# The recurrence of a hybrid layer stack: half-array products in pairs, small inversions on GpSimd

## The chip, the cores and the metric

The kernel runs on one core of one Trainium2 chip, in one launch. The metric is the device time of one launch in microseconds; three runs of the kernel before gave 2369.61, 2371.10 and 2373.16 us, median 2371.1 us.

The engines are named as in the profile: PE is the matrix engine (TensorE, its weight loads are shown as PEld), DVE is VectorE, ACT is ScalarE, POOL is GpSimd, SP is the engine whose queue issues nearly all transfers of this kernel.

## The reference, cut to what matters

Two blocks follow each other on 256 tokens of 1024 features. The second block's first layer has a mixer with two halves: grouped attention, and a two-directional recurrence over 256 context and 256 latent tokens with 8 heads of 64 features (the two directions of a head run over the tokens in opposite order). The change lies in the recurrence alone:

```python
w_log = w0 + einsum('btdr,drc->btdc', tanh(wl), w2)      # d: the two directions, r: 64
decay = exp(-exp(-softplus(-w_log) - 0.5))
a = sigmoid(a0 + einsum('btdr,drc->btdc', al, a2))
k_dir = k * (1 + (a - 1) * k_a)
def step(S, inp):                                          # once per token, one 64x64 state per head
    r, w, k, v, kk, a = inp
    S = S * w - (S @ kk)[:, None] * (kk * a) + v[:, None] * k
    return S, S @ r
```

## The kernel before

All numbers are float32. The stack is a chain of matrix products whose weights stream from HBM; each weight tile is split into a high and a low part (`split`, L97 and L98) and each product runs as three passes (`mm3`, L115 to L117). These products fill most of the span. The recurrence lies between about 880 and 1195 us.

**Units.** The recurrence does not step through tokens. It cuts the 512 tokens into four tiles of 128, each of two chunks of 64, and works on eight units, one per tile and direction. For each unit four functions run:

- the first half of `rwkv_in` (the *front*): it loads the two low-rank inputs of the tile into `wa` (one transfer, L1463; direction 0 uses the partitions 0 to 63, direction 1 the partitions 64 to 127, `db`), multiplies with `rwkv_w2` for the decay (L1466, 64 rows of the array, 512 columns wide), sums the logarithms over the chunk with a triangular product (L1479), takes exponentials (L1481, L1482), and multiplies with `rwkv_a2` for the rate `a` (L1488, four products on the same 64 rows) followed by tanh on ACT (L1493). All three products use the one PSUM bank `fr`, one after the other;
- the second half of `rwkv_in` (the *back*): it scales keys and queries on DVE (L1507 to L1519) and then forms the 64x64 Gram matrices of eight heads in two chunks (L1529). For a chunk `ch` and a parity `q` of the head, four products on 64 rows (`half(q)`: partitions 0 to 63 or 64 to 127) write the one PSUM bank `gg`; then DVE multiplies that bank with a mask into SBUF (L1533). So there are four groups of four products per unit, two on each row half, and `gg` is filled and emptied four times. Between them `fill` puts pieces of the attention half into the program. Afterwards two sets of transposes on `gg` (L1544) are copied out by ACT (L1545);
- `rwkv_solve`: the diagonal 16x16 blocks of the Gram matrices go to HBM (`dq`, L1540), come back as 64 lanes of 16x16 (`dl`, L1560), are inverted by 14 pairs of small multiply and add (L1565, L1566: 64 partitions by at most 56 columns, each dependent on the one before; the profile shows them under the helper's line L120 with the tiles `dt` and `dl`), and go back to HBM (`dy`, L1568). The multiplies and adds are DVE's, the two transfers are SP's;
- `rwkv_maps`: it reads the blocks back (`x`, L1589), transposes them on DVE (L1590) and completes the 64x64 inverses by 64x64 products on all four quarters of the array (`each`, L1595), then builds each chunk's map of the state (`lw`, L1637, L1651). `lw` and `si` are buffers of 128x1024 that are cleared once by POOL (L1280, L1284).

Then `rwkv_step` carries the state through the chunks (L1669, L1678).

**Order.** The list `GA` (L22) writes out the order of the first units beside the projections of the same layer; `rwkv` (L1272) then runs, for each `n`: back of unit n, front of unit n+2, solve of unit n, maps of unit n-2, and steps after every second one. `rate` (L355, values `FT` and `FE`) says how many pieces of attention `fill` puts at each point. The framework then plans each engine's queue by these priorities and by when operands and buffers come free, so that the pieces of several functions alternate on an engine. Each queue runs in order; an instruction that waits holds up all behind it on its engine.

**PSUM.** Eight banks. While the recurrence runs, `fr` and `wm` have one each; `wm` serves the modulation products of other stages and is not used in this one.

Of the kernel before, what the change touches and what calls it, by code (L numbers as in the profile page):

```python
# [14 lines left out]
AF = mybir.ActivationFunctionType  # L15
# [31 lines left out]
@with_exitstack  # L47
def kernel(ctx: ExitStack, tc: tile.TileContext, A: dict, out: bass.AP, taps=None):
    nc = tc.nc
    V, S, E = nc.vector, nc.scalar, nc.tensor  # L50
    taps = taps or {}

    cpool = ctx.enter_context(tc.tile_pool(name="cpool", bufs=1))
# [1024 lines left out]
    def even_mixer(l, en):  # L1078
        T = 512
        close_psum()  # L1080
        with tc.tile_pool(name=nm("em"), bufs=1) as pk, tc.tile_pool(name=nm("rf"), bufs=2) as fp, \
                tc.tile_pool(name=nm("emd"), bufs=1, space=bass.MemoryType.DRAM) as dp:
            open_psum(fr=1, wm=1)
            open_psum(mm=3, sc=1, tr=1, gg=1)

            def dram(name, *shape):
# [1 line left out]

            D = dict(q=dram("qd", 4, 8, 128), k=dram("kd", 4, 512), vv=dram("vvd", 4, 128), o=dram("oTd", 8, 512), g=dram("gd", 4, 512), x=en.store, f=dram("fd", 12, 512), lo=dram("lod", 3, 512), v=dram("vd", 4, 512))
            rc = const("rcols", pk)  # L1090
            C = {n: const(n, pk) for n in ("rwkv_w2", "rwkv_a2", "rtri", "gmask", "tmask", "eye2", "sgn")}
            a0 = const("rwkv_a0", pk)
            C["ha0"] = pk.tile([128, 2, 4], F32, tag="ha0", name="ha0")
            ts(C["ha0"], a0, 0.5)
# [177 lines left out]
    def rwkv(C, D, order, stages, bon, yac):  # L1272
        front, back, solve = stages
        with tc.tile_pool(name=nm("rk"), bufs=1) as pk:
            eye2 = C["eye2"]
            C["lw"] = []
            for n in range(2):
                C["lw"].append([pk.tile([128, 4, 4, 64], F32, tag=f"lw{n}{ch}", name=nm("lw")) for ch in range(2)])
                for ch in range(2):
                    nc.gpsimd.memset(C["lw"][n][ch], 0.0)  # L1280
            si = []
            for n in range(2):
                x = pk.tile([128, 2, 2, 4, 64], F32, tag=f"si{n}", name=nm("si"))
                nc.gpsimd.memset(x, 0.0)  # L1284
                for par in range(2):
                    hb = half(1 - par)
                    for d in range(2):
                        acopy(x[hb, d, par], eye2[hb].unsqueeze(1).to_broadcast([64, 4, 64]))
                si.append(x)

            with tc.tile_pool(name=nm("ru"), bufs=2) as up, tc.tile_pool(name=nm("rw"), bufs=1) as wk, tc.tile_pool(name=nm("at"), bufs=1) as ap:
                stream[0] = merge(ORDER, iter(()), even_attention(D, ap, ("sc", "tr", "tr")))
                C["up"][1], C["wk"] = up, wk
                tm = gate_consts(D, pk)
                side = iter(())

                def steps(p):
                    tiles = ((2, 3), (0, 1))[p // 2]
                    z = {(un["d"], un["t"]): un["z"] for un in order[4 * (p // 2):2 * p + 2]}
                    for n in (0, 1) if p % 2 == 0 else (2, 3):  # L1300
                        yield from rwkv_step(n, tiles, z, si, yac)

                ahead = 2
                for n in range(8 + ahead):
                    rate[:] = FE.get(n, FT)
                    if n < 8:
                        for do, what in zip((back, front, solve), "bfs"):
                            u = n + 2 * (what == "f")
                            if u < 8 and (what, u) not in GA:
                                do(u)  # L1310
                    if n >= ahead:
                        u = n - ahead
                        for _ in rwkv_maps(C, D, order[u]):
                            fill(rate[3])
                            next(side, None)
                        if u % 2:
                            for _ in steps(u // 2):
                                fill(rate[4])
                            if u == 3:
                                side = itertools.chain(*(g for t in (2, 3) for g in (gates(D, bon, tm, t), readout(D, tm, t, yac[:, t % 2], True))),  # L1320
                                                       *(gates(D, bon, tm, t) for t in (0, 1)))
                for _ in side:
                    fill(FR)
                drain()
# [128 lines left out]
    def rwkv_in(fp, C, D, un):  # L1453
# [5 lines left out]
        def w512(tag, shape=(128, 4, 128), pool=fp, bufs=None):  # L1459
            return pool.tile(list(shape), F32, tag=tag, name=nm(tag), **({"bufs": bufs} if bufs else {}))  # L1460

        wa = w512("wa", (128, 2, 128))
        nc.sync.dma_start(out=wa[db], in_=D["lo"][db, 0:2, tok])  # L1463

        ps = pst("fr")
        E.matmul(out=ps, lhsT=wa[db, 0], rhs=C["rwkv_w2"][db, :], start=True, stop=True)  # L1466
        sg = w512("sg", (128, 512), bufs=1)
        nc.sync.dma_start(out=sg, in_=A["rwkv_w0"][:, d])
        tt(sg, ps, sg, ALU.add)
# [13 lines left out]
        inc, exc = eo[:, :, :, 1 - d:65 - d], eo[:, :, :, d:64 + d]  # L1483
        pc = eo[:, :, :, 64 - first]

        ps = pst("fr")
        for f in range(4):
            E.matmul(out=ps[:, f * 128:(f + 1) * 128], lhsT=C["rwkv_a2"][db, f * 128:(f + 1) * 128], rhs=wa[db, 1], start=True, stop=True)  # L1488

        ak = w512("ak", (128, 4, 4, 64))  # L1490
        at, kd = ak[:, :, 0:4:3], ak[:, :, 1:3]
        for f in range(4):
            S.activation(out=at[:, f], in_=ps[:, f * 128:(f + 1) * 128].rearrange("p (c t) -> p c t", c=2), func=AF.Tanh, scale=0.5, bias=C["ha0"][:, d, f:f + 1])  # L1493
            S.activation(out=kd[:, f], in_=at[:, f], func=AF.Identity, scale=C["kah"][:, 0, f:f + 1], bias=C["kah"][:, 1, f:f + 1])
        S.activation(out=at, in_=at, func=AF.Copy, scale=0.5, bias=0.5)
        yield
# [25 lines left out]
        g = w512("g", (128, 8, 2, 192), up)  # L1522
        for ch in range(2):
            cc = slice(ch * 64, ch * 64 + 64)
            for q in range(2):
                ps = pst("gg")
                for h in range(4):
                    f, hb = h, half(q)
                    E.matmul(out=ps[:, h * 128:(h + 1) * 128], lhsT=ak[hb, f].rearrange("p a t -> p (a t)")[:, ch * 128:ch * 128 + 128],  # L1529
                             rhs=ar[hb, f, 1:3, cc], start=True, stop=True)  # L1530
                if q or ch:
                    fill(rate[0])
                tt(g[:, q:8:2, ch, 64:192], ps.rearrange("p (h t) -> p h t", h=4),  # L1533
                   gmask[:, d, ch].unsqueeze(1).to_broadcast([128, 4, 128]), ALU.mult)
        if d == 1:
            gt = fe[:, 8:12].rearrange("p n (a t) -> p (n a) t", a=2)
# [2 lines left out]
        for ch in range(2):  # L1539
            nc.sync.dma_start(out=rows_of(dq, ch), in_=gt[half(ch)] if d == 1 else g[half(ch), :, ch, 128:192])  # L1540
        for ch in range(2):
            ps = pst("gg")
            for j in range(4):
                E.transpose(ps[:, j * 128:(j + 1) * 128], bk.rearrange("p f a t -> p f (a t)")[:, j, ch * 128:(ch + 1) * 128], ident)  # L1544
            S.activation(out=g[:, :, ch, 0:64], in_=ps.rearrange("p (h t) -> p h t", h=8), func=AF.Copy, scale=C["sgn"][:, ch:ch + 1])  # L1545
# [10 lines left out]
    def rwkv_solve(C, un):  # L1556
        wk = C["us"]

        y = wk.tile([64, 16, 16], F32, tag="dl", name=nm("dl"), bufs=2)
        nc.sync.dma_start(out=y, in_=lanes_of(un["dq"]))  # L1560
        for c in range(1, 15):
            n = 15 - c
            tmp = wk.tile([64, 64], F32, tag="dt", name=nm("dt"), bufs=2)
            o = tmp[:, :c * n].rearrange("p (a r) -> p a r", a=c)
            tt(o, y[:, 0:c, c].unsqueeze(2).to_broadcast([64, c, n]), y[:, c, c + 1:16].unsqueeze(1).to_broadcast([64, c, n]), ALU.mult)  # L1565
            tt(y[:, 0:c, c + 1:16], y[:, 0:c, c + 1:16], o, ALU.add)  # L1566
        V.memset(y.rearrange("p a r -> p (a r)")[:, 0:256:17], 1.0)
        nc.sync.dma_start(out=lanes_of(un["dy"]), in_=y)  # L1568

    def rwkv_maps(C, D, un):  # L1570
        d, t, u, dy, ar, g = (un[n] for n in ("d", "t", "u", "dy", "ar", "g"))
# [299 lines left out]
def _layout(x):  # L1871
# [35 lines left out]
    o["rows_g"] = _rows(x["q_gain_2"], x["k_gain_2"])  # L1907
    o["rwkv_mu"] = _cols(x["rwkv_mu_2"][0])
    o["rwkv_w0"] = np.broadcast_to(x["rwkv_w0_2"], (128, 2, 512))
    o["rwkv_w2"] = x["rwkv_w2_2"][0].reshape(128, 512)  # L1910
    o["rwkv_a0"] = _cols(x["rwkv_a0_2"][0])
    o["rwkv_a2"] = x["rwkv_a2_2"][0].reshape(128, 512)
    o["rwkv_g2"] = x["rwkv_g2_2"][0]
    o["rcols"] = _cols(np.stack([x["rwkv_k_k_2"][0], x["rwkv_k_a_2"][0], x["rwkv_r_k_2"][0].reshape(512)]))
    o["gn"] = np.broadcast_to(np.stack([x["rwkv_gn_w_2"][0], x["rwkv_gn_b_2"][0]]), (128, 2, 512))
# [29 lines left out]
```

## Time and profile before

| | |
|---|---|
| runs | 2369.61, 2371.10, 2373.16 us |
| profiled execution | 2372.83 us, span 2371.0 us |
| PE busy | 2272.9 us (96%), 13642 matrix instructions |
| DVE busy | 1570.0 us (66%) |
| ACT busy | 1069.8 us (45%) |
| POOL busy | 5.6 us, 10 instructions |
| mean granted clock of PE | 0.97 |

The profile is of one execution. Each float32 product shows as two PE records. The time of a stretch is given from the span's start. A record of PE has a measured start and a modelled end, so starts are what to compare. The chain is the sequence of work that ended last, followed back from the end: at each step what released it. DMA issues show on the issuing engine's queue (SPq); "to landing" is the time from the issue to the arrival of the data.

### The profile page before, as it was taken

Reading aid. Unit: us, or ns where it says so; the run is one execution under the profiler, and the core shown is the slowest. Engines: PE = TensorE matmul, PEld = TensorE weight load, DVE = VectorE, ACT = ScalarE, POOL = GpSimd, SP = SyncE. Lnnn points to the kernel's source line nnn. Section 1 sums busy time; section 2 is a strip of 40 time slices with the busy share of each in tenths; the row PEclk is TensorE's granted clock in tenths of the full one; section 3 lists DMA queues with packets and bytes.
Section 4 is the critical chain, followed back from the end, with each engine's and each line's share of the span. In section 5 each row is a group of like instructions: output and inputs, shape, how many; then the busy total and the mean of one; then the engine's idle time right before and its main releaser. Section 6 shows DMA issues by size and latency. Waiting matters only on the chain.

```text
span 2371.0 us, 35433 instructions
## 1 busy us (share of the span) xinstructions
PE 2272.9 (96%) x13642; PEld 1856.6 (78%) x13642; DVE 1570.0 (66%) x3074; ACT 1069.8 (45%) x1882; POOL 5.6 (0%) x10
## 2 busy tenths in 40 slices
PE   8999999999999998998878999999999999999998
PEld 6688797778787786876767878787778788768998
DVE  7867779667835766878678677437754334787555
ACT  6756666322224637564535222224422223476444
POOL 0000000000000000000000000000000000000000
PEclk9999998999999998999979999999999999999999
DMA  8556444545524445332354555323553222314553
GB/s 294 176 183 218 164 154 161 188 162 182 180 94 130 144 147 141 90 87 60 92 189 140 169 181 183 124 91 120 175 183 132 90 98 90 103 36 136 181 184 118
DMA packets 161962, 342.02 MB, mean 144 GB/s; under 512 B 48513, under 2 KB 76161, under 8 KB 161665
## 3 DMA queue, kind: packets, MB, share of 16 engines
q1 hardware_dynamic: 161072, 339.15, 43.7%
q8 instruction: 108, 1.77, 0.3%
q10 hardware_dynamic: 720, 0.60, 0.1%
q14 instruction: 62, 0.50, 0.1%
HBM read 321.86 MB, written 17.84 MB: 143 GB/s over the span
## 4 chain that ended last, share of the span: by engine, by line
PE 89%; DVE 5%; ACT 3%; DMA 1%; issue 1%; SPq 0%; DVEq 0%; ACTq 0%
PE mm L115 25%; PE mm L117 24%; PE mm L116 24%; PE gg L1529 2%; PE m L1595 1%; PE tr L219 1%; PE m L1651 1%; DVE wlo L98 1%; PE wm L331 1%; PE po L1056 1%; PE wm L274 1%; PE tr L1056 1%; ACT whi L97 1%; PE po L541 1%; PE sc L1010 1%
## 5 line engine op out<-in xcount | busy, mean ns | idle before, releaser
L97 ACT CAST whi<-raw 128x1024 fp32r<-128x1024 f32 (+2 forms) x437 | 437.4, 1002 | 988.9 <-PE mm L116 596.1
L115 PE MATMUL mm<-xh,whi 128*128 128x512 f32 (+1 forms) x1912 | 680.8, 360 | 16.5 <-ACT xh L97 9.5
L117 PE MATMUL mm<-xh,wlo 128*128 128x512 f32 (+1 forms) x1912 | 679.2, 357 | 5.2 <-DVE wlo L98 5.0
L116 PE MATMUL mm<-xl,whi 128*128 128x512 f32 (+1 forms) x1912 | 680.4, 357 | 1.2 <-DVE xl L98 1.1
L98 DVE TENSOR_TENSOR wlo<-raw,whi 128x1024 fp32r<-128x1024 f32 (+2 forms) x437 | 507.5, 1163 | 256.0 <-ACT whi L97 249.5
L115 PEld LDWEIGHTS mm<-xh,whi 128*128 128x128 f32 x1912 | 365.1, 192 | 82.2 <-ACT whi L97 16.4
L117 PEld LDWEIGHTS mm<-xh,wlo 128*128 128x128 f32 x1912 | 365.3, 191 | 57.8 <-DVE wlo L98 7.1
L116 PEld LDWEIGHTS mm<-xl,whi 128*128 128x128 f32 x1912 | 365.4, 191 | 53.8 <-DVE xl L98 4.2
L117 PE MATMUL mm<-hh,wlo 128*128 128x512 f32 (+1 forms) x704 | 260.0, 369 | 0.0
L116 PE MATMUL mm<-hl,whi 128*128 128x512 f32 (+1 forms) x704 | 258.0, 367 | 0.1
L115 PE MATMUL mm<-hh,whi 128*128 128x512 f32 (+1 forms) x704 | 257.0, 366 | 0.0
L129 DVE SCALAR_TENSOR_TENSOR macc<-raw,modc,macc 128x1024 f32<-128x1024 f32 x189 | 234.3, 1278 | 0.5
L129 DVE SCALAR_TENSOR_TENSOR xres<-mm,mod,xres 128x256 f32<-128x256 f32 x216 | 96.2, 479 | 167.1 <-PE mm L117 166.8
L120 DVE TENSOR_TENSOR fg<-mm,fg 128x512 f32<-128x512 f32 (+1 forms) x84 | 52.4, 623 | 161.5 <-PE mm L117 160.9
L115 PEld LDWEIGHTS mm<-hh,whi 128*128 128x128 f32 x704 | 132.0, 188 | 27.8 <-issue 2.5
L116 PEld LDWEIGHTS mm<-hl,whi 128*128 128x128 f32 x704 | 132.3, 188 | 26.1 <-DVE hl L98 0.7
L115 PE MATMUL mm<-whi,xh 128*128 128x512 f32 (+1 forms) x360 | 143.6, 404 | 9.1 <-ACT whi L97 8.5
L117 PEld LDWEIGHTS mm<-hh,wlo 128*128 128x128 f32 x704 | 132.4, 188 | 22.8
L116 PE MATMUL mm<-wlo,xh 128*128 128x512 f32 (+1 forms) x360 | 143.8, 400 | 2.8 <-DVE wlo L98 2.8
L117 PE MATMUL mm<-whi,xl 128*128 128x512 f32 (+1 forms) x360 | 142.3, 397 | 0.0
L115 PEld LDWEIGHTS mm<-whi,xh 128*128 128x128 f32 x360 | 68.5, 192 | 31.3 <-ACT whi L97 9.8
L116 PEld LDWEIGHTS mm<-wlo,xh 128*128 128x128 f32 x360 | 68.9, 191 | 17.2 <-DVE wlo L98 5.3
(396 smaller groups left out, 2540.5 us busy)
## 6 DMA issues: line engine op xcount, KB each, us to landing
raw<-in_ffn_in SPq DMA_DIRECT2D x176, 512.0 KB, 3.6
raw<-in_w_mod SPq DMA_DIRECT2D x144, 512.0 KB, 4.4
raw<-in_ffn_out SPq DMA_DIRECT2D x64, 448.0 KB, 3.2
raw<-in_w_in_even SPq DMA_DIRECT2D x32, 512.0 KB, 4.9
raw<-in_w_in_odd SPq DMA_DIRECT2D x32, 512.0 KB, 4.1
raw<-in_ffn_out SPq DMA_DIRECT2D x32, 512.0 KB, 3.5
raw<-in_w_ple_gate SPq DMA_DIRECT2D x16, 512.0 KB, 4.3
raw<-in_even_r SPq DMA_DIRECT2D x15, 512.0 KB, 3.5
```

Source lines behind the costliest of these rows:

```text
L97: S.copy(out=hi, in_=src)
L98: V.tensor_tensor(out=lo, in0=src, in1=r32(hi), op=ALU.subtract)
L115: E.matmul(out=ps, lhsT=ah, rhs=bh, start=first, stop=False)
L116: E.matmul(out=ps, lhsT=ah, rhs=bl, start=False, stop=False)
L117: E.matmul(out=ps, lhsT=al, rhs=bh, start=False, stop=last)
L120: V.tensor_tensor(out=o, in0=a, in1=b, op=op)
L129: V.scalar_tensor_tensor(out=o, in0=a, scalar=s, in1=b, op0=op0, op1=op1)
L219: E.transpose(ps[:, j * 128:(j + 1) * 128], s, ident)
L274: E.matmul(out=ps[32 * j:32 * j + 32, hf * 256:hf * 256 + 256], lhsT=cz[:, 4 * g + j, 10 - 2 * c:42 - 2 * c], rhs=raw[:, j], start=c == 0 ...
L331: E.matmul(out=ps[32 * j:32 * j + 32], lhsT=mod_1[:, 2 - q:34 - q], rhs=acc[:, v, hf * 512:hf * 512 + 512], start=q == 0, stop=q == 2)
L1056: E.matmul(out=po[half(a), 0:256], lhsT=vt[:, j], rhs=pt[:, j, 2 * a:2 * a + 2], start=j == 0, stop=j == nk - 1)
L1529: E.matmul(out=ps[:, h * 128:(h + 1) * 128], lhsT=ak[hb, f].rearrange("p a t -> p (a t)")[:, ch * 128:ch * 128 + 128], rhs=ar[hb, f, 1:3, ...
```

## The change

1. **Products in pairs.** The two matrices `rwkv_w2` and `rwkv_a2` become one constant `rwkv_wa`, whose partitions 0 to 63 hold `w2` and 64 to 127 hold `a2`, for both directions. `wa` becomes 128x128 and is loaded by two transfers, one per half. The front issues the decay product (rows 0 to 63, bank `fr`) and directly behind it the four products for `a` (rows 64 to 127, a new bank `gh`). The back issues the four products of `q = 0` and of `q = 1` alternately, into `gg` and `gh`, and empties the two banks after that; so there are two groups of eight per unit. The second set of transposes uses `gh`. `gh` takes the place of `wm` in PSUM.
2. **Solve on GpSimd.** The 28 multiplies and adds of a unit, the clearing of the diagonal, and the two transfers `dl` and `dy` are issued by POOL.
3. **Clears on VectorE.** The six clears of `lw` and `si` go from POOL to DVE.

```diff
-            open_psum(fr=1, wm=1)
+            open_psum(fr=1, gh=1)
...
-            C = {n: const(n, pk) for n in ("rwkv_w2", "rwkv_a2", "rtri", "gmask", "tmask", "eye2", "sgn")}
+            C = {n: const(n, pk) for n in ("rwkv_wa", "rtri", "gmask", "tmask", "eye2", "sgn")}
...
-                    nc.gpsimd.memset(C["lw"][n][ch], 0.0)
+                    V.memset(C["lw"][n][ch], 0.0)
...
-                nc.gpsimd.memset(x, 0.0)
+                V.memset(x, 0.0)
...
-        wa = w512("wa", (128, 2, 128))
-        nc.sync.dma_start(out=wa[db], in_=D["lo"][db, 0:2, tok])
-        ps = pst("fr")
-        E.matmul(out=ps, lhsT=wa[db, 0], rhs=C["rwkv_w2"][db, :], start=True, stop=True)
+        wa = w512("wa", (128, 128))
+        for j in range(2):
+            nc.sync.dma_start(out=wa[half(j)], in_=D["lo"][db, j, tok])
+        ps, pa = pst("fr"), pst("gh")
+        E.matmul(out=ps, lhsT=wa[half(0)], rhs=C["rwkv_wa"][half(0), d], start=True, stop=True)
+        for f in range(4):
+            E.matmul(out=pa[:, f * 128:(f + 1) * 128], lhsT=C["rwkv_wa"][half(1), d, f * 128:(f + 1) * 128], rhs=wa[half(1)], start=True, stop=True)
...
-        ps = pst("fr")
-        for f in range(4):
-            E.matmul(out=ps[:, f * 128:(f + 1) * 128], lhsT=C["rwkv_a2"][db, f * 128:(f + 1) * 128], rhs=wa[db, 1], start=True, stop=True)
...
         for ch in range(2):
             cc = slice(ch * 64, ch * 64 + 64)
+            pq = pst("gg"), pst("gh")
+            for f in range(4):
+                for q in range(2):
+                    hb = half(q)
+                    E.matmul(out=pq[q][:, f * 128:(f + 1) * 128], lhsT=ak[hb, f].rearrange("p a t -> p (a t)")[:, ch * 128:ch * 128 + 128],
+                             rhs=ar[hb, f, 1:3, cc], start=True, stop=True)
             for q in range(2):
-                ps = pst("gg")
-                for h in range(4):
-                    f, hb = h, half(q)
-                    E.matmul(out=ps[:, h * 128:(h + 1) * 128], lhsT=ak[hb, f].rearrange("p a t -> p (a t)")[:, ch * 128:ch * 128 + 128],
-                             rhs=ar[hb, f, 1:3, cc], start=True, stop=True)
                 if q or ch:
                     fill(rate[0])
-                tt(g[:, q:8:2, ch, 64:192], ps.rearrange("p (h t) -> p h t", h=4),
+                tt(g[:, q:8:2, ch, 64:192], pq[q].rearrange("p (h t) -> p h t", h=4),
                    gmask[:, d, ch].unsqueeze(1).to_broadcast([128, 4, 128]), ALU.mult)
...
-            ps = pst("gg")
+            ps = pst(("gg", "gh")[ch])
...
-        nc.sync.dma_start(out=y, in_=lanes_of(un["dq"]))
+        P.dma_start(out=y, in_=lanes_of(un["dq"]))
...
-            tt(o, y[:, 0:c, c].unsqueeze(2).to_broadcast([64, c, n]), y[:, c, c + 1:16].unsqueeze(1).to_broadcast([64, c, n]), ALU.mult)
-            tt(y[:, 0:c, c + 1:16], y[:, 0:c, c + 1:16], o, ALU.add)
-        V.memset(y.rearrange("p a r -> p (a r)")[:, 0:256:17], 1.0)
-        nc.sync.dma_start(out=lanes_of(un["dy"]), in_=y)
+            P.tensor_tensor(out=o, in0=y[:, 0:c, c].unsqueeze(2).to_broadcast([64, c, n]), in1=y[:, c, c + 1:16].unsqueeze(1).to_broadcast([64, c, n]), op=ALU.mult)
+            P.tensor_tensor(out=y[:, 0:c, c + 1:16], in0=y[:, 0:c, c + 1:16], in1=o, op=ALU.add)
+        P.memset(y.rearrange("p a r -> p (a r)")[:, 0:256:17], 1.0)
+        P.dma_start(out=lanes_of(un["dy"]), in_=y)
```

## Rows read from the trace of the kernel before

**Rows 1.** The page, part 4: shares of the span in the chain, by engine.
```profile
PE 89%; DVE 5%; ACT 3%; DMA 1%; issue 1%; SPq 0%; DVEq 0%; ACTq 0%
```

**Rows 2.** Stretches of the recurrence: length, busy time (instructions) by engine, clock, DMA share, GB/s.
```profile
880.00:935.00 55.00, 52.50 (x304) 39.92 (x302) 39.75 (x112) 39.60 (x100) 0.00 (x0) 1.00 0.44 133
935.00:952.00 17.00, 11.72 (x34) 7.33 (x35) 11.40 (x38) 13.77 (x40) 5.40 (x6) 0.51 0.74 155
952.00:1100.00 148.00, 141.78 (x1850) 115.36 (x1849) 120.75 (x322) 91.42 (x211) 0.00 (x0) 0.98 0.35 88
1100.00:1150.00 50.00, 41.59 (x538) 32.14 (x540) 39.71 (x116) 22.95 (x44) 0.00 (x0) 0.90 0.29 74
1150.00:1200.00 50.00, 37.90 (x519) 31.20 (x514) 29.01 (x62) 24.97 (x56) 0.00 (x0) 0.84 0.31 96
```

**Rows 3.** PE's groups by line and shape, 880 to 1200: count, busy us, mean ns.
```profile
L1529 PE MATMUL gg<-ar,ak 64*128 64x128 f32 x256 | 39.9, 300 | 3.8 <-DVE g L120 2.2 <-DVE ak L120 1.5
L1466 PE MATMUL fr<-rwkv_w,wa 64*128 64x512 f32 x16 | 9.9, 703 | 0.0
L1488 PE MATMUL fr<-wa,rwkv_a 64*128 64x128 f32 x64 | 9.7, 287 | 0.3 <-ACT ei L1482 0.3
```

**Rows 4.** PE in order of time (start, us), 903.2 to 904.6.
```profile
903.45 1.16 PE L1529 MATMUL gg<-ar,ak 64*128 64x128 f32 x8
```

**Rows 5.** PE in order of time, 929.9 to 931.5.
```profile
930.16 0.37 PE L1488 MATMUL fr<-wa,rwkv_a 64*128 64x128 f32 x1 [0.28 <-ACT ei L1482]
930.17 0.37 PE L1529 MATMUL gg<-ar,ak 64*128 64x128 f32 x1
...
931.16 0.27 PE L1488 MATMUL fr<-wa,rwkv_a 64*128 64x128 f32 x1
```

**Rows 6.** PE in order of time, 58.5 to 62 and 70 to 73.
```profile
58.92 0.49 PE L602 MATMUL sc<-qk,qk 64*128 64x128 f32 x4
...
70.15 0.48 PE L602 MATMUL sc<-qk,qk 64*128 64x128 f32 x2
```

**Rows 7.** PE's waits, 880 to 1200: us in total, times, longest.
```profile
PE sc L1010 <- ACT gp L1013: 8.0, 7, 2.3
...
PE gg L1544 <- ACT g L1545: 2.4, 3, 0.8
PE gg L1529 <- DVE g L120: 2.2, 3, 0.8
```

**Rows 8.** DVE's groups by line, 900 to 1200.
```profile
L120 DVE TENSOR_TENSOR dt<-dl 64x14 f32<-64x14 f32 (+6 forms) x112 | 20.8, 185 | 1.1 <-DMA dl<-dq 0.2
L120 DVE TENSOR_TENSOR dl<-dl,dt 64x14 f32<-64x14 f32 (+6 forms) x112 | 20.6, 183 | 0.9
```

**Rows 9.** Lines L1560, L1568, L1589, L1590: ns min/median/max, first and last start.
```profile
L1560 SPq DMA_DIRECT2D dl<-dq x8: 592/594/833, 915.1 to 1120.1; - x8
L1568 SPq DMA_DIRECT2D dy<-dl x8: 575/588/596, 936.1 to 1144.4; - x8
L1589 SPq DMA_DIRECT2D x<-dy x16: 574/627/1536, 942.6 to 1148.2; - x16
L1590 DVE STREAM_TRANSPOSE x<-x x8: 684/694/711, 954.2 to 1152.6; 128x512 f32<-128x512 f32 x8
```

**Rows 10.** DMA issues by line: KB each, median us to landing.
```profile
x<-dy SPq DMA_DIRECT2D x16, 128.0 KB, 3.5
...
dl<-dq SPq DMA_DIRECT2D x8, 64.0 KB, 4.3
```

**Rows 11.** Groups by line of POOL, then of DVE's clears, whole span.
```profile
L1280 POOL MEMSET lw<- 128x1024 f32 x4 | 3.6, 952 | 934.6 <-DVE dt L120 934.6
...
L1928 POOL MEMSET const-float32-0.0<- 128x1 f32 x1 | 0.1, 99 | 0.2 <-issue 0.2
...
L780 DVE MEMSET bz<- 128x256 f32 x5 | 1.4, 272 | 0.0
```

**Rows 12.** Sum over four stretches at half clock (934.5:951.6, 955:961.8, 1101.8:1112, 1183.7:1200.8).
```profile
sum 51.20, PE 36.10 PEld 26.21 DVE 34.44 ACT 22.37 POOL 5.40; mean PE 9.03 PEld 6.55 DVE 8.61 ACT 5.59 POOL 1.35
```

More of the change, by code (lines that the diff above doesn't have):

```diff
@@ L49 @@
     nc = tc.nc
-    V, S, E = nc.vector, nc.scalar, nc.tensor
+    V, S, E, P = nc.vector, nc.scalar, nc.tensor, nc.gpsimd
     taps = taps or {}
@@ L1492, in rwkv_in @@
         for f in range(4):
-            S.activation(out=at[:, f], in_=ps[:, f * 128:(f + 1) * 128].rearrange("p (c t) -> p c t", c=2), func=AF.Tanh, scale=0.5, bias=C["ha0"][:, d, f:f + 1])
+            S.activation(out=at[:, f], in_=pa[:, f * 128:(f + 1) * 128].rearrange("p (c t) -> p c t", c=2), func=AF.Tanh, scale=0.5, bias=C["ha0"][:, d, f:f + 1])
             S.activation(out=kd[:, f], in_=at[:, f], func=AF.Identity, scale=C["kah"][:, 0, f:f + 1], bias=C["kah"][:, 1, f:f + 1])
@@ L1909, in _layout @@
     o["rwkv_w0"] = np.broadcast_to(x["rwkv_w0_2"], (128, 2, 512))
-    o["rwkv_w2"] = x["rwkv_w2_2"][0].reshape(128, 512)
+    o["rwkv_wa"] = np.concatenate([x["rwkv_w2_2"][0].reshape(2, 64, 512).transpose(1, 0, 2), x["rwkv_a2_2"][0].reshape(2, 64, 512).transpose(1, 0, 2)], 0)
     o["rwkv_a0"] = _cols(x["rwkv_a0_2"][0])
-    o["rwkv_a2"] = x["rwkv_a2_2"][0].reshape(128, 512)
     o["rwkv_g2"] = x["rwkv_g2_2"][0]
```

## The prediction

> **What bounds the kernel now.** I read the chain first: PE carries 89% of it and DVE 5% [rows 1], so a change pays where it takes time from PE or lets PE stop waiting. Next come the stretches of the recurrence [rows 2]. From 880 to 1100 PE is busy 206.0 of 220 us; in its long middle part, 952 to 1100, it is 141.8 of 148, beside a DVE at 120.8 (82%). There PE's own work sets the pace and DVE is the next limit. From 1100 to 1200 PE is busy only 79.5 of 100 us: the attention pieces that filled the gaps run out and latencies show. Then I asked which PE work the change touches, by line and shape [rows 3]: the Gram products L1529 take 39.9 us, the decay product L1466 9.9, the rate product L1488 9.7, together 59.5 us of products that use 64 of 128 array rows. Last I read PE's waits: in 320 us the longest is for the softmax on ACT (8.0 us), and those for a Gram or transpose bank are 2.2 and 2.4 us [rows 7]. So waits are short and work is long.
>
> **What a pair of row halves is worth.** A group of four products on one half, alone, is eight records in 1.16 us [rows 4]. The trace has a place where two such groups happen to stand side by side: at 930.16 L1488 starts on one half, at 930.17 L1529 on the other, they alternate, and the sixteenth record starts at 931.16 and takes 0.27 [rows 5]. So 16 records take 1.27 us where two groups alone take 2.32: 1.05 us saved per pair of groups. The first layer writes pairs on purpose (L602: two heads' halves into two banks); at 58.92 four records need 0.49 us, but at 70.15 two records alone need 0.48 [rows 6]: there one half came without the other, because its bank was not free. A pair pays only when both banks are free at once.
>
> **The Gram products.** Eight units by two chunks make 16 pairs: at most 16 x 1.05 = 16.8 us. The first chunk's pair finds `gg` and `gh` long empty, and I take it whole: 8 x 1.05 = 8.4 us. The second chunk's pair needs both banks emptied by DVE, and the second emptying stands behind the first and behind pieces of attention; if `gg` comes free first, the products of one half can go ahead alone. I take half: 4.2 us. Two of the eight units fall mostly in the stretch after 1100, where PE has idle time and not all of the saving shortens the span: minus 1.0. Together 11.6 us, between 6 and 16.8.
>
> **The front's products.** L1466 and L1488 are 9.9 + 9.7 = 19.6 us; as pairs of 1.27 they would be 10.2, so 9.4 us at most. Some of this is already had: the group of rows 5 ran beside Gram products, and such overlaps are lost when the product moves. I bound it by 7. Also `pa` waits for `gh`, which the back's second transposes hold until ACT has copied them; a decay product that goes ahead then runs alone. I take half of the 7: 3.5 us, between 0 and 7. The second `wa` transfer costs SP 0.6 us eight times (the small transfers' issue in rows 9), against sixteen such issues that leave SP; nothing on the path.
>
> **The new waits on PE.** Transposes of the second chunk no longer wait for ACT's copy of the first: minus 2.4 us [rows 7]. Against it, the second pair waits for two emptyings where a group now waits for one. Behind it in PE's queue are attention pieces and the maps' products, and DVE and ACT wait for those. I put this at the present 2.2 us once more: plus 2 (0 to 5).
>
> **The solve leaves DVE.** 112 + 112 instructions of 185 and 183 ns, 20.8 + 20.6 = 41.4 us of DVE [rows 8], 5.2 us per unit. Little of it is on the path by itself, since it is fitted between other DVE work; what it buys is that bank emptyings, softmax reductions and the scaling ahead of the Gram products come sooner. PE's waits that this can shorten are the 8.0 and 2.2 us of rows 7. I take 3 us, between 0 and 10.
>
> **The solve on POOL.** The trace shows no arithmetic and no transfer on POOL. What it must not exceed can be read. From the issue of `dl` to the issue of `dy` the first unit needs 936.1 - 915.1 = 21.0 us and the last 1144.4 - 1120.1 = 24.3 (the first and the last of eight) [rows 9], of which 4.3 is the read [rows 10] and the rest 28 DVE steps spread among other work. Behind it, the first unit's second read of `x` (one issue of about 0.6 after 942.6, landing 3.5 later: 946.7) has 7.5 us to spare before its transpose at 954.2; the last unit's (1148.2 + 3.5 = 1151.7, transpose at 1152.6) has 0.9 [rows 9, 10]. I take the middle, 22.7 us with 4.2 to spare: a unit may take 26.9. On POOL it takes 4.3 + 28 p, plus what its own issue of two transfers costs beyond SP's. For p the nearest rows are DVE's same step, 0.18 us [rows 8], POOL's clear of one column, 0.10, and of 1024 columns, 0.95 [rows 11]; a step has at most 56 columns but reads two operands and depends on the step before. I take 0.3, nearest to DVE's, with 0.10 and 0.95 as ends, and 1 us more per transfer (0 to 4, the top being the landing time of rows 10): 4.3 + 8.4 + 2 = 14.7 us. It is covered, and worth nothing on the path: 0.
>
> The Trainium skill, page "GPSIMD Engine Reference", section 3 "Performance versus the Vector engine", speaks against this part: it calls GpSimd the wrong choice for elementwise work and gives 1.96 times DVE's time for a large add. Twice DVE's 0.18 us would be an estimate, by that page, of 0.37 us a step and 10.4 us for 28, and the sum would be the same. No row here has such a step on POOL, so only the profile of the changed kernel can decide.
>
> **The clears on DVE.** Six clears of 1024 columns: four times 0.272 is 1.09 us each, 6.5 in all; POOL's same clear took 0.95, 5.7 in all [rows 11]. They fall near 935 to 952, where DVE is busy 11.4 of 17 us [rows 2] and also loses the solve. Cost 0; with that room gone, up to 6.
>
> **Clock.** Four stretches of the recurrence, 51.2 us, ran at the lower clock (1.2 of 2.4 GHz), with PE busy 36.1 us [rows 12]; about half of that, 18 us, is what the lower clock costs, 4.5 per stretch. PE had gaps before them. I count none won or lost, and one stretch either way, 4.5 us, in the range.
>
> **Sum.** -11.6 - 3.5 - 2.4 + 2 - 3 = -18.5 us. Against the profiled execution's own 2372.8 us that is 2354.3; the median of the runs, 2371.1, lies 1.7 lower. I predict 2354.
>
> **Rivals.**
> *The pairs come apart.* For: rows 6 show it, and `gg` and `gh` are emptied one after the other by one engine. Then half of the first chunks' pairs are left, 4.2 us, no front pair, and the same relief and waits: 4.2 + 2.4 + 3 - 2 = 7.6, so 2365. Against: rows 5, where 16 records interleave without being planned.
> *VectorE is held up by POOL.* If each of 224 steps of 0.3 us kept DVE from working for its length, DVE would lose 67 us and be given 41.4: 26 us more than now on an engine at 82% in the middle stretch. The 3 us of relief go, and the 8.0 + 2.2 us of rows 7 double: 2354 + 3 + 10 = 2367, no measurable change. The Trainium skill, page "SBUF — State Buffer", section "Who interferes with whom", states such a lock: a VectorE instruction with two SBUF operands and a GpSimd instruction that reads SBUF block each other, the later one fully. The clears of rows 11 only write, so nothing in this trace tests it. Against its full price: many of DVE's instructions here read PSUM.
> *The solve comes too late.* The place is the wait of the maps (L1590, and the products L1595 behind it) for `x`. It begins at 26.9 us per unit and eats the whole gain of 18.5 / 8 = 2.3 us per unit at 29.2, which is p = (29.2 - 4.3 - 2) / 28 = 0.82 us. At the upper end, p = 0.95, a unit takes 32.9, 6.0 us late eight times: 48 - 18.5 = 29.5 us slower than before, 2402. For: the last unit has 0.9 us to spare, and 28 steps each wait for the one before. Against: a clear of 18 times as many columns takes 0.95.
>
> **How the numbers follow.** The forecast (pairs mostly whole, solve covered) has 0.56, with its own range 2342 to 2364. Pairs apart 0.16, VectorE held up 0.13, solve too late 0.15. The range reaches down to all terms at their best (16.8 + 7 + 2.4 + 10 = 36, 2337) and up into the late solve at p near 0.85 (2380), and leaves out the rest of that case, some 0.1. What this kernel's measurement can tell from no change is about 0.2%, 4.7 us. Faster by more: 0.54 of the forecast, 0.11 of the pairs apart, 0.06 of the rest: 0.71. Within: 0.02 + 0.05 + 0.06 + 0.03 = 0.16. Slower: 0.03 + 0.10 = 0.13.
>
> **What would show it.** Right: L1529's records in couples some 10 ns apart on opposite halves, sixteen in about 1.3 us, its busy time near 23 to 28 us; DVE without `dt` and `dl` and about 70% or less busy in the middle stretch; POOL's solve from `dl` to `dy` under 21 us and L1590 no later after `x` than now. Wrong: groups of eight records of one half in a row (pairs apart); DVE's two-operand instructions longer than before while POOL runs (held up); PE or DVE waiting on `x` with POOL busy until just before (late). Above all I would be wrong if POOL's step is near a microsecond, since no row bounds it closely.

## The result, and the profile after

The changed kernel takes 2389.1 us (median of four runs), the kernel before 2371.5 beside it: ratio 1.0072, interval 1.0056 to 1.0088, so 18 us slower where 18.5 us faster was forecast. The profiled execution took 2387.4 us, its span 2385.6. In the profiles all of it arises in the recurrence: the last state product starts at 1192.8 us before and 1208.1 after.

First, the page: busy time by engine, then the shares of the chain. [rows 1] of before has PE at 89% and no POOL.

```profile
PE 2261.1 (95%) x13642; PEld 1846.1 (77%) x13642; DVE 1548.3 (65%) x2848; ACT 1073.4 (45%) x1884; POOL 97.1 (4%) x252
...
PE 84%; DVE 5%; DMA 3%; ACT 3%; POOL 2%; issue 2%; SPq 0%; DVEq 0%; POOLq 0%; ACTq 0%
```

PE has 11.8 us less work than before, and the kernel is still longer: PE waits more. The stretches of [rows 2], with the last one longer by 15 us (columns as there; the last three are the granted clock, the DMA share and GB/s):

```profile
880.00:935.00 55.00, 50.71 (x310) 38.59 (x308) 36.46 (x89) 45.47 (x109) 13.57 (x36) 0.98 0.46 128
935.00:952.00 17.00, 6.15 (x39) 4.40 (x40) 14.23 (x21) 9.94 (x31) 10.97 (x27) 0.55 0.67 195
952.00:1100.00 148.00, 128.91 (x1716) 101.69 (x1718) 96.42 (x171) 86.64 (x201) 49.38 (x125) 0.94 0.31 79
1100.00:1150.00 50.00, 35.13 (x389) 27.09 (x386) 32.34 (x63) 21.98 (x39) 22.96 (x61) 0.86 0.20 52
1150.00:1215.00 65.00, 51.81 (x782) 42.35 (x781) 38.64 (x80) 32.39 (x70) 0.00 (x0) 0.88 0.32 98
```

In the middle stretch PE falls from 141.8 to 128.9 us, DVE from 120.8 to 96.4 (65%): both have room, so a latency sets the pace. The pairs are what the change says. PE in order of time, unit 0's first chunk (the first two of sixteen records, and the last):

```profile
902.80 0.37 PE L1531 MATMUL gg<-ar,ak 64*128 64x128 f32 x1
902.81 0.37 PE L1531 MATMUL gh<-ar,ak 64*128 64x128 f32 x1
...
903.69 0.27 PE L1531 MATMUL gh<-ar,ak 64*128 64x128 f32 x1
```

Sixteen records span 0.89 us from first to last start and 1.16 to the end, as long as eight took in [rows 4]. All of L1531 in the recurrence, both banks, is this (one row for 880 to 1215; 39.91 us before, [rows 3]):

```profile
880.00:1215.00 335.00, 26.96 (x256) 21.80 (x256) 0.91 0.34 93
```

Then who waits. The longest waits of SP's queue, of DVE and of PE, 880 to 1215 (engine, line, what it waited for: us in total, times, longest), and last SP's same wait in the kernel before:

```profile
SPq L1592 <- DMA dy<-dl: 48.5, 7, 12.3
...
DVE x L1593 <- DMA x<-dy: 19.8, 5, 7.8
DVE ro L120 <- DMA ro<-vd: 13.9, 2, 10.4
...
PE gg L1547 <- DVE g L120: 10.5, 1, 10.5
PE gg L1531 <- DVE ar L120: 8.3, 1, 8.3
PE y L1672 <- ACT g L223: 6.7, 3, 5.4
PE m L1598 <- DVE T L120: 5.9, 1, 5.9
PE y L1672 <- DVE yac L120: 5.1, 2, 3.5
...
SPq L1589 <- DMA dy<-dl: 12.1, 5, 4.8
```

L1592 (before: L1589) is SP's read of `x`, L1593 DVE's transpose of it. Before, DVE never waited for `x`. Yet POOL is not slow: from the issue of `dl` (911.1) to that of `dy` (927.4) the first unit takes 16.3 us and the last 14.6 (1130.6 to 1145.2), against 21.0 and 24.3 of DVE [rows 9]. Lines L1563 and L1571 (ns min/median/max, first and last start):

```profile
L1563 POOL DMA_DIRECT2D dl<-dq x8: 832/833/966, 911.1 to 1130.6; - x8
...
L1571 POOL DMA_DIRECT2D dy<-dl x8: 852/854/864, 927.4 to 1145.2; - x8
```

What happens shows at units 4 and 5. DVE, then SP, in order of time:

```profile
1043.91 0.68 DVE L120 TENSOR_TENSOR g<-gh,gmask 128x512 f32<-128x512 f32 x1
1044.62 0.71 DVE L1541 STREAM_TRANSPOSE fe<-g 64x512 f32<-64x512 f32 x1
1053.11 0.71 DVE L1593 STREAM_TRANSPOSE x<-x 128x512 f32<-128x512 f32 x1 [7.78 <-DMA x<-dy]
...
1048.87 0.58 SPq L1592 DMA_DIRECT2D x<-dy  x1
...
1050.18 0.61 SPq L1592 DMA_DIRECT2D x<-dy  x1
1050.95 0.59 SPq L1543 DMA_DIRECT2D dq<-fe  x1
...
1052.25 0.60 SPq L1543 DMA_DIRECT2D dq<-fe  x1
1055.24 0.55 SPq L1500 DMA_DIRECT2D fe<-fd  x1
```

Unit 5's blocks are ready at 1045.3. SP's queue has the read of unit 4's `x` ahead of their write; it stands there until unit 4's `dy` has landed (issued 1046.1), so `dq` goes out at 1050.95 and 1052.25, and the load of the next `fe` behind it. DVE meanwhile waits 7.78 us for the same `x`. Unit 5's solve (`dl` at 1055.4) begins only after unit 4's has been read. So solves that overlapped, from the write of `dq` to the read of `x`, now follow one another.

PE's four long gaps after 950 us hang on the same places. Three end just behind a transpose that DVE waited for (PE waits 5.4, 5.9 and 3.5 us, from 1004, 1048 and 1079). The longest, 10.5 us from 1114, comes by SP's queue: the load of `ro` stands behind the reads of unit 6's `x`, and the masks of unit 7's second chunk stand behind `ro` on DVE. The chain there (start, us, what):

```profile
1114.45 2.72 DMA dy<-dl
1117.23 0.58 SPq L1592
...
1118.54 0.61 SPq L1592
...
1119.24 3.86 DMA ro<-vd
...
1123.12 0.69 DVE ro L120
```

The four gaps add up to 25 us. From 950 to 1160 neither the kernel before nor the run with the pairs alone (below) has one over 2 us.

In the queues of before, the writes of `dq` of units 2, 3, 5 and 7 stand ahead of the reads of `x` of units 1, 2, 4 and 6; now all stand behind them (of unit 3 one of two). From a unit's last mask to its transpose of `x`, DVE had 23 to 36 us of other work and 6.7 to 9.4 us of solve steps before; now it has 15 to 28 us of other work (its rows between the two, added up). The way from the last `dq` over POOL to `x` takes 25 to 29 us (37 for the first unit): 3 from the issue of `dq` to that of `dl`, 4.2 to its landing, 11 to 14 for the steps, 3 for `dy` and 4 for `x`. That is shorter than before, when it took 30 to 42.

The theory, **places**: the plan, made anew, put the reads and transposes of `x` earlier in SP's and DVE's in-order queues than their data comes, ahead of the next unit's work. Rivals: the path over POOL is too **long** wherever it is read; the **shared port** slows DVE; POOL's **transfers** are slow; the **pairs** or the **clears** cost the time.

### The profile page after: what moved, and what is told of

Read it like the earlier page. It is cut to its first block, busy times and chain, and to the rows that moved or that the text cites. A ratio compares the mean times of both kernels' runs of the same rounds, so it can differ in the third digit from the quotient of the medians.

```text
span 2385.6 us, 35469 instructions
## 1 busy us (share of the span) xinstructions
PE 2261.1 (95%) x13642; PEld 1846.1 (77%) x13642; DVE 1548.3 (65%) x2848; ACT 1073.4 (45%) x1884; POOL 97.1 (4%) x252
## 4 chain that ended last, share of the span: by engine, by line
PE 84%; DVE 5%; DMA 3%; ACT 3%; POOL 2%; issue 2%; SPq 0%; DVEq 0%; POOLq 0%; ACTq 0%
PE mm L115 24%; PE mm L117 24%; PE mm L116 24%; PE tr L219 1%; DVE wlo L98 1%; POOL dl L1569 1%; POOL dt L1568 1%; DMA dl<-dq 1%; PE m L1598 1%; PE wm L274 1%; PE wm L331 1%; PE po L1056 1%; DMA x<-dy 1%; ACT whi L97 1%; PE po L541 1%
```

## Experiments

### Parts alone

`e1_pairs`: solve and its transfers back on DVE and SP, clears back on POOL.

```diff
-        P.dma_start(out=y, in_=lanes_of(un["dq"]))
+        nc.sync.dma_start(out=y, in_=lanes_of(un["dq"]))
-            P.tensor_tensor(out=o, ...)
+            V.tensor_tensor(out=o, ...)
...
-                    V.memset(C["lw"][n][ch], 0.0)
+                    nc.gpsimd.memset(C["lw"][n][ch], 0.0)
```

> The change with the solve back on DVE and its two transfers on SP, and the clears back on POOL: of the change only the pairs are left. If the pair terms of the prediction are right (Gram pairs -11.6, front pairs -3.5, transposes -2.4, the new wait +2), this runs 15.5 us faster than before: about 2356 us, between 2346 and 2365. If the pairs or the shared bank gh are what cost the 18 us (rival: pairs), it is as slow as the changed kernel, 2380 to 2390; if they bring nothing, 2371.

Measured: 2352.1 us, ratio to the kernel before 0.991 (0.9892 to 0.9927): 20 us faster. The pairs gain more than forecast; they are not the cause.

`e2_solve`: the kernel before with the change's `rwkv_solve`, nothing else.

> The kernel before with the solve (28 steps a unit and both transfers) on POOL, no pairs, clears on POOL. Theory (the result of a solve reaches x later than SP's read and DVE's transpose stand in their queues): the changed kernel is 18 us slower with pairs that gain some 15 and clears that cost up to 6, so the solve by itself costs 27 to 33 us: 2398 to 2404. Rival (the solve hurts only where the pairs have made PE quicker): 2371 to 2380. Rival (the move of the solve is covered, as predicted): 2366 to 2371.

Measured: 2391.8 us, 1.0077 (1.0062 to 1.0092): 20 us slower, less than the 27 to 33 expected. The two parts don't add up: -20 and +20 make +18, so beside the pairs the solve, with the clears, costs 37 us. This kernel and the changed one end at about the same time: when the solves set the pace, PE's shorter work is worth nothing. SP's wait ahead of `x` is 64.3 us here, DVE's 24.9.

`e3_no_clears`: the change with `V.memset` of `lw` and `si` back to `nc.gpsimd.memset`.

> The change with only the six clears back on POOL. If the clears cost what their place in the chain shows (six times 1.12 us, start to start, in a gap of PE of 8.3 us): 2389 - 6.5 = about 2382.5. If DVE waited there for fe anyway (4.6 us of wait just before them): 2387 to 2389. A rival is that POOL's clears then delay the first solve's dl read: 2389 or more.

Measured: 2392.4 us, 1.0083 (1.0066 to 1.01). No gain, where 6.5 us were expected if the clears cost their place in the chain. POOL and SP in order of time show what the clears meet on POOL:

```profile
949.26 3.64 POOL L1280 MEMSET lw<- 128x1024 f32 x4
...
950.26 1.47 SPq L1577 DMA_DIRECT2D lw<-vd  x2
```

The clears stand behind unit 1's solve in POOL's queue, SP waits 10 us for them ahead of `lw` (issued at 950.26), and the second half of unit 0's `x` is read at 951.8 instead of 942.2. In its profile PE reaches record 4836 (of the table below) 5 us sooner than in the change and record 4900 6 us later, so the gain is lost right there.

`e4_sp_moves`: as that, with `dl` and `dy` issued by `nc.sync` again.

> As the run with the clears on POOL, but the solve's two transfers are SP's again; only its 28 steps stay on POOL. Compared with that run: if POOL's way of issuing transfers is what makes the result late (rival: transfers), most of the loss goes, 10 to 20 us faster than it; if the steps and the places of the reads do it, within 4 us of it; SP would then also stand behind the issue of dy, so a little slower is possible (up to 10).

Measured: 2417.0 us, 1.0184 (1.0169 to 1.02), 25 us slower than with POOL's transfers, more than the 10 allowed for. Its longest wait of SP:

```profile
SPq L1571 <- POOL dl L1569: 86.7, 8, 12.9
```

SP stands before `dy` until POOL's steps are done, with everything else behind it. `e8_dl_pool` is the counterpart, pairs with the steps on DVE, the clears on POOL, and only the two transfers moved to POOL:

> The pairs, the 28 steps on DVE and the clears on POOL as before, but the transfers dl and dy issued by POOL. If POOL's way of issuing transfers is what makes the solve late: 2360 to 2375, against 2352 with SP's. If not: 2346 to 2354, a little better at best, since SP issues sixteen fewer and no longer waits for the steps ahead of dy.

Measured: 2355.5 us, 0.9926 (0.9909 to 0.9944), within 4 us of the pairs alone, just above what was expected and below the 2360 of the rival. POOL's transfers are not the cause.

### Places

`e5_late`: for units 0 to 5, the transpose of unit u queued behind the first mask of unit u+2, an order without a wait.

```diff
-        V.transpose(flat(x[d]), flat(x[1 - d]))
...
+            with tc.issue_after(un["later"]["mk"][0]):
+                V.transpose(flat(x[d]), flat(x[1 - d]))
```

> The changed kernel with one order added: DVE's transpose of x of unit u (L1593) is queued behind the first mask of unit u+2, which is where the kernel before has most of them; nothing else is fixed, the transfers stay where the plan puts them. Theory (places: on DVE the transpose, on SP the reads of x stand ahead of the next unit's Gram masks and of its dq writes, so the solves of successive units follow one another instead of overlapping): DVE's 19.8 us of waits for x go, SP's 48.5 us of waits ahead of x stay in part, so part of the 38 us that the solve costs beside the pairs comes back: 2365 to 2380. Rival (length: the path over POOL is too long wherever its result is read): 2385 to 2395, the wait only moves.

Measured: 2373.5 us, 1.0007 (0.9997 to 1.0016). 16 us come back, as expected of places.

`e6_xpool`: `P.dma_start` instead of `nc.sync.dma_start` for `x` (L1592).

> The changed kernel with the two reads of x per unit issued by POOL, behind its own write of dy, instead of SP. Theory (places, SP's part): SP no longer stands before x, so the next unit's dq, its fe and lw loads and the attention's queries go out in time: of SP's 48.5 us of waits most go, 2362 to 2378; DVE's early transposes remain. Rival (only DVE's place counts): 2385 to 2390. Rival (POOL's way of issuing is the slow part): slower than the changed kernel, over 2392.

Measured: 2403.6 us, 1.0124 (1.0101 to 1.0147): 14.5 us slower than the change, against my expectation, and in the range of the rival that POOL's way of issuing is slow. DVE's wait in it:

```profile
DVE x L1593 <- DMA x<-dy: 47.3, 8, 9.8
```

SP no longer stands before `x`, but DVE's wait for it grew from 19.8 to 47.3 us: the transposes still stand early, and DVE now waits at every unit. `e7_late_xpool` is both edits:

> Both at once: the transpose behind the first mask of unit u+2, and the reads of x on POOL. Theory (places): the solve on POOL is then covered as the prediction had it, and the pairs' gain shows: about 2352 (the run with the pairs alone) less up to 3 of DVE relief, 2345 to 2358. Rival (length or shared port): 2375 or more.

Measured: 2368.5 us, 0.9984 (0.9973 to 0.9995), between the two expectations, 10 us above the theory's. It is 5 us faster than with the late transposes alone, so reads issued by POOL are not slow in themselves. DVE hardly waits (3.5 us), but for units 0 to 5 `x` lies 21 to 36 us between its issue and its transpose. What that lateness costs is not shown.

The next three use the places of the run with the pairs alone. `e11_sp_order` pins SP's reads of `x` for units 1 to 6, `e10_dve_order` DVE's transposes for units 0 to 6, `e9_as_pairs` both:

```diff
+    DP = {0: ("ar", 2), 1: ("bk", 3), 2: ("z", 1, 3), 3: ("mk", 4, 1), 4: ("z", 3, 1), 5: ("mk", 6, 3), 6: ("up", 5)}
+    SPP = {1: ("fe", 3), 2: ("fe", 4), 3: ("lw", 3, 1), 4: ("fe", 6), 5: ("lw", 5, 1), 6: ("dq", 7, 1)}
...
+            with behind(SPP.get(un["n"])):
                 nc.sync.dma_start(out=x[1 - d][half(ch)], in_=rows_of(dy, ch))
+        with behind(DP.get(un["n"])):
             V.transpose(flat(x[d]), flat(x[1 - d]))
```

> The changed kernel with the places of the run with the pairs alone (2352 us): DVE's transpose of x for units 0 to 6 is queued behind the same instruction that stood before it there (the scaling of unit 2's queries, the last scaling of unit 3, a sum of unit 1's map, the second mask of unit 4, ...), and SP's reads of x behind the transfers that they followed there (fe of units 3, 4 and 6, lw of units 3 and 5, dq of unit 7). The solve stays on POOL and the clears on DVE. Theory (places): the transposes stand where the solve is ready, neither early as in the change nor late as behind the masks of unit u+2 (x then lay 20 to 37 us unused): 2350 to 2360. Rival (the rest of the loss, 16 us after the two earlier orders, is the solve's own length or the shared port): 2368 or more.

Measured: 2365.4 us, 0.9965 (0.9954 to 0.9976).

> Only DVE's half of those places; SP's reads of x stand where the plan puts them. If DVE's place is what matters and SP's follows from it: 2352 to 2364. If SP's place decides by itself: 2375 to 2389.

Measured: 2373.4 us, 1.0003 (0.9993 to 1.0013).

> Only SP's half of those places. If SP's reads of x, which stand ahead of the next unit's dq, make the solves follow one another: 2360 to 2375. If DVE's early transposes alone do it: 2385 to 2392; later reads of x can then only make DVE wait longer.

Measured: 2367.1 us, 0.997 (0.9957 to 0.9983). SP's places alone return 22 of the 37 us and DVE's 16; both together return 24, no clear gain over SP's. That is what was expected of SP's places. DVE's order came out between its two expectations, and so did the two together, which left 13 us over the pairs alone. In the run with SP's places, SP at units 4 and 5:

```profile
1039.15 2.65 SPq L1551 DMA_DIRECT2D dq<-fe  x2
...
1044.49 1.63 SPq L1601 DMA_DIRECT2D x<-dy  x2
```

and its waits, SP's and then DVE's:

```profile
SPq L1585 <- PE m L1664: 41.6, 8, 12.8
SPq L1601 <- DMA dy<-dl: 13.7, 3, 8.2
...
DVE x L1603 <- DMA x<-dy: 5.1, 2, 3.9
```

Unit 5's `dq` now goes out ahead of unit 4's `x` (the issues end at 1041.8, in the change at 1052.9), and the writes of units 2, 3 and 7 are back ahead of the reads too. PE's longest gap from 950 to 1160 is 3.2 us, where the change has the four that add up to 25. SP still waits 41.6 us, for a buffer of `lw`, in a run that is 22 us faster: not how long a queue waits decides here, but what stands behind the waiting instruction. The pins let the plan move other instructions as well; a run that moves these reads and nothing else was not made.

`e12_half_steps`: `for c in range(1, 15, 2)`.

> The changed kernel with every second column of the inversion left out: 14 steps a unit on POOL instead of 28, the transfers and the wait for them as they are (part of the inverse is not computed). 14 steps of 0.35 us are 4.9 us a unit. Theory (the solves follow one another and set the pace in most units): five to eight units get 4.9 us shorter, 2349 to 2365. Rival (the loss comes from the shared port, which slows DVE's instructions): the two-operand instructions on DVE meet half as many steps, half of the slowing goes, under 8 us: 2381 or more.

Measured: 2371.7 us, 0.9997 (0.9985 to 1.0008), 17.5 us faster than the change, between the two expectations. From `dl` to `dy` a unit takes 11.0 us on average against 17.2, so 6.2 us, not the 4.9 expected, count at about three units. SP's wait falls from 48.5 to 20.9 us. So the length does act while the solves follow one another. The shared port alone, which was given under 8 us, does not explain it; and the run with SP's places has the same 28 steps on POOL without most of the loss.

### The clears

Where the rest arises: the start of PE's n-th record of the span, and how much later each profiled execution reaches it than the pairs alone do (us, from the records' starts).

```
record   pairs alone   change   SP's places   SP's places, clears first
4794        925         -1.5       -1.1              -2.3
4836        941          6.1        6.7              -0.2
5532       1000         12.6        7.8               3.6
6150       1045         18.8        6.0               1.1
6833       1105         30.3        5.0               2.2
7296       1135         33.8       10.1               8.2
```

With SP's places, 7.8 of 10 us arise at 925 to 941. The last column is the slowest of that run's four executions, 5 us above their median. The changed kernel's PE and DVE there:

```profile
938.17 1.22 DVE L120 TENSOR_TENSOR ak<-ak,ei 128x1024 f32<-128x1024 f32 x1
939.55 0.91 DVE L1280 MEMSET lw<- 128x1024 f32 x1 [0.16 <-DMA x<-dy]
...
944.92 0.91 DVE L1284 MEMSET si<- 128x1024 f32 x1 [0.16 <-issue]
945.75 1.24 DVE L120 TENSOR_TENSOR ar<-fe,eo 128x512 f32<-128x512 f32 x2
...
947.05 0.58 PE L1531 MATMUL gg<-ar,ak 64*128 64x128 f32 x1 [8.34 <-DVE ar L120]
```

The six clears stand in the middle of the scaling that the Gram products wait for: 939.55 to 945.83, 6.3 us of an 8.34 us gap of PE. Two runs put them on POOL ahead of unit 1's steps (`s1`, unit 1's solve, leaves the written-out order and is called behind the clears); the first of them also has SP's places:

```diff
-GA = "l0 q0 r0 r1 r2 r3 k0 f0 v0 b0 s0 f1 f2 b1 f3 s1 v1 v2 v3"
+GA = "l0 q0 r0 r1 r2 r3 k0 f0 v0 b0 s0 f1 f2 b1 f3 v1 v2 v3"
-                V.memset(x, 0.0)
+                C["last"] = nc.gpsimd.memset(x, 0.0).ins
...
+            if c == 1 and un["n"] == 1:
+                hold = tc.issue_after(C["last"])
```

> SP's reads of x in the places of the run with the pairs alone, and the six clears on POOL again, but ahead of unit 1's 28 steps there (its solve is then called after them and queued behind the last clear). Against the run with SP's places alone (2367): theory (its remaining 15 us over the pairs alone are mostly the clears, which on DVE stand before the scaling of unit 2 in a gap of PE of 8.3 us): 6 to 9 us faster, 2356 to 2362. Rival (the remainder is the solve's length): 2364 or more, since unit 1's solve now begins some 6 us later.

Measured: 2357.3 us, 0.9934 (0.9916 to 0.9951), 9.8 us less than with SP's places alone by the medians, 8.5 by the ratios, as expected.

> The changed kernel with the clears on POOL ahead of unit 1's steps, and nothing else. With the clears on POOL behind unit 1's steps it was no faster than with them on DVE (2392 against 2389). If that was because SP's loads of lw and the read of x behind them had to wait until POOL had done unit 1 (second read of unit 0 at 951.8 instead of 942.2 us), then this order gives the price of the clears on DVE: 2389 - 6.5 = 2382, between 2376 and 2386. If the clears on DVE cost nothing on the path: 2387 to 2393.

Measured: 2389.7 us, 1.0068 (1.0051 to 1.0085): nothing, against my expectation. In its profile PE is 4.5 us ahead of the change at record 4836 and 4 us behind it at record 5200. The clears put off unit 1's steps, so that its `dy` is issued at 955.3 us instead of 947.4, and DVE's wait for `x` grows from 19.8 to 37.8 us. So while the solves follow one another the gain is lost again, to a later solve. With SP's places unit 1's `dy` is as late (953.7) and the gain stays: there the clears on DVE cost 8 to 10.

## Why the prediction was wrong

**The step that failed** is "The solve on POOL": "a unit may take 26.9 ... It is covered, and worth nothing on the path: 0". The solve took 14.6 to 19.0 us from `dl` to `dy`, at or above the 14.7 forecast and well under the 26.9 allowed. What was wrong is the allowance. I read from [rows 9] where the transposes of `x` stand, and took those places as fixed. The 4.2 us to spare were a fair reading (over the eight units it was 1.3 to 9.1, 4.7 on average). But this kernel's queues are planned, and the move changed the plan: the reads and transposes of `x` moved forward, ahead of the next unit's `dq`. The same solve, with the clears, costs 37 us in the new places, 15 with SP's reads in the old ones, and 5 when the clears are out of the way too (2357.3 against 2352.1; the intervals overlap a little). In that last run's profile PE has one long gap left between 950 and 1160 us, at the last unit, whose `x` no run pinned:

```profile
DVE x L1608 <- DMA x<-dy: 6.6, 2, 5.1
...
PE tr L1028 <- DVE gp L124: 4.4, 1, 4.4
```

The transpose (here L1608) again stands early on DVE, which waits 5.1 us for `x` until 1126.6, and the scaling of `gp` that PE waits for until 1127.9 stands behind it. So the rest looks like the same fault at unit 7; no run moved it.

**The rival "the solve comes too late"** named the right place, the maps' wait for `x`, but tied it to a step of 0.82 us. The step was 0.28 us at the median, 0.37 on average. No rival had the queue's order in it, and the measured time lies above the range.

**The pairs.** Gram products: -13.0 us of PE (39.91 to 26.96), forecast -11.6. With the front, the transposes and the new wait I had -15.5; the run with the pairs alone gave -20, with PE 20.8 us less busy. Part of this may be the clock, which I counted at nothing: from 880 to 1215 it was 0.94 there and 0.92 before. It stands behind PE and PEld in the rows of the Gram products, before and with the pairs alone:

```profile
880.00:1215.00 335.00, 39.91 (x256) 33.58 (x256) 0.92 0.40 108
880.00:1215.00 335.00, 26.55 (x256) 21.85 (x256) 0.94 0.42 116
```

**The clears.** "Cost 0; with that room gone, up to 6": the room was gone, 6.3 us in the gap, 8 to 10 measured once the solves overlap. Six in-order instructions landed in front of the scaling; their busy time was sized well (6 x 0.91, and 1.07 from start to start), their place was not asked for.

**The clock.** I counted nothing won or lost by it. The changed kernel's granted clock was 0.94 in the middle stretch, where before had 0.98, and 0.86 in the one behind it, where before had 0.90. Its four falls to half (1.2 of 2.4 GHz) between 1008 and 1118 us each begin in one of PE's four long gaps or less than 1 us after it. They hold 27 us at half clock, 10 of them in the gaps themselves; half of the rest, some 8 us by this estimate, is the most that they add to the waits.

**VectorE held up by POOL.** DVE was relieved: 65% busy in the middle stretch, as forecast. POOL's steps lengthen DVE's two-operand instructions only a little. The scaling of the queries and the last scaling, first with the pairs alone, then in the change (groups of 950 to 1150; count, busy us, mean ns):

```profile
L120 DVE TENSOR_TENSOR ar<-fe,eo 128x512 f32<-128x512 f32 x10 | 6.7, 673 | 0.0
L120 DVE TENSOR_TENSOR fe<-ak,eo 128x1024 f32<-128x1024 f32 x5 | 6.1, 1210 | 0.0
...
L120 DVE TENSOR_TENSOR ar<-fe,eo 128x512 f32<-128x512 f32 x10 | 7.0, 715 | 0.0
L120 DVE TENSOR_TENSOR fe<-ak,eo 128x1024 f32<-128x1024 f32 x5 | 6.3, 1260 | 0.0
```

Some 40 to 50 ns each, 0.7 us over these fifteen, far from the 67 us that this rival took as its ceiling. That relief of DVE bought time was not shown: no kernel with the solve on POOL beat the pairs alone, which is the best version found.

## What to carry to other kernels

Where queues are planned from dependences, moving a step to another engine moves the instructions around it as well: before covering a step's new latency with the old timetable, ask which queue holds its reader, and what stands behind that reader. Two chains that should overlap stop doing so when one in-order queue holds the read of the first ahead of the start of the second; reordering that queue was worth more here (22 us) than halving the chain's steps (17.5). While such a loop sets the pace, gains elsewhere can measure as nothing, as the pairs' did, so undo the parts one by one and again together.

## What the runs showed of the hardware

A small dependent two-input step on 64 partitions takes POOL 0.2 to 0.3 us by itself, against DVE's 0.18 [rows 8], and several times that when it meets a two-operand instruction of DVE. POOL's multiplies by line (count, busy us, mean ns), then POOL and DVE in order of time:

```profile
L1568 POOL TENSOR_TENSOR dt<-dl 64x14 f32<-64x14 f32 (+6 forms) x112 | 42.0, 375 | 36.8 <-DMA dl<-dq 28.6
...
995.71 1.15 POOL L1569 TENSOR_TENSOR dl<-dl,dt 64x50 f32<-64x50 f32 x1
...
995.41 1.31 DVE L120 TENSOR_TENSOR ak<-ak,ei 128x1024 f32<-128x1024 f32 x1
```

The step of 995.71 ends just after DVE's instruction (996.72), at 996.86. Of the 45 steps longer than 0.4 us, 43 overlap a DVE instruction with two operands in SBUF; of the other 179, 13 do. Over 224 steps the mean is 0.37 us against a median of 0.28, some 20 us in all, borne by POOL. This agrees with the rule of the Trainium skill, page "SBUF — State Buffer", section "Who interferes with whom", that the two share a port pair under an exclusive lock. The factor of 1.96 of the Trainium skill, page "GPSIMD Engine Reference", section 3 "Performance versus the Vector engine", fits the mean (0.37 / 0.18 = 2.0), not the median step (0.28 / 0.18 = 1.5). The mean holds the blocked steps, so that it fits may be chance.

POOL's issue of a transfer of 1024 runs of 64 bytes holds it 0.83 to 0.85 us, SP's 0.6 [rows 9]; the read lands after 4.2 us, as SP's did [rows 10].
